# Pinning ScalarE's casts and the gate's tanh to the order of the source in a two-pipe transformer mixer

## The chip, the cores and the metric

The kernel runs on one core of one Trainium2 chip. The metric is device time in microseconds of one launch. The engines named below are TensorE (PE: matmuls and transposes), VectorE (DVE), ScalarE (ACT: casts, exponentials, tanh), GpSimd (POOL) and SyncE (SP, which issues most transfers); each works its own queue from front to back and waits on semaphores for the others.

## The reference

One layer of an encoder over a prompt of 2048 tokens and 8 sample streams of 16 tokens each, 1024 wide:

```python
h   = RMSNorm(x)
z   = h @ w_in     # one combined projection, columns split among head groups
A   = chunk-band attention   # 8 heads x 64: own chunk of 64 and 8 before it, learned bias
B   = mLSTM matrix memory    # 4 heads x 128: exp input gate, sigmoid forget gate, running max
x   = x + RMSNorm(concat(RMSNorm_A(A), sigmoid(o) * headRMSNorm_B(B)) @ w_out)
x   = x + RMSNorm(ConvFFN(RMSNorm(x)))   # up, causal depthwise conv of width 3, GELU gate, down
```

The attention's score is `s = q k / 8 + bias`, masked to the band, then a softmax over the keys and a product with the values. Everything is fp32.

## The kernel before

Each fp32 operand of a matmul is split in two parts: a cast to fp32r on ScalarE gives the high part, a subtraction on VectorE the low part, and three matmuls (`mm3`, lines 95 to 97: high x high, high x low, low x high) give the product. So almost every transfer of an operand is followed by a cast on ScalarE and a subtraction on VectorE before TensorE may read it. Those casts are what the change is about.

The mixers (roughly the first 1100 us of the span; then come the out-projection and the ConvFFN) are built round 28 projection groups, 14 for each half of the prompt, in the order of `GROUPS`: `va` are the attention's values, `qk` its queries and keys, `qb` the queries and keys of the memory, `vo` its values and output gate. A group's weights (512 KB in each of two halves) come through `load_group`. It is called for the next group while the current one runs, and is stepped inside its loop: fetch half 0 into the raw buffer `wraw` (one buffer), cast a quarter (`wi.._h`, L1175) and subtract (`wi.._l`, L1176), then the second quarter, then the same for half 1. A quarter holds two of the eight 128-row blocks of the weights. The results of a group accumulate in two PSUM banks (`ps_mm`), are copied out by ScalarE (L224, L226) and go to DRAM.

Between the matmuls of a group, `pump` inserts steps of two `Pipe`s by a running count of estimated TensorE and VectorE costs. One pipe is the attention: for each head `load_head` fetches queries, keys and values and casts them (`qs` L342, `kh` L346, `vhl` L355). For each tile of 128 queries `att_unit` makes scores `s` (L382, L383), adds the bias and takes the row minimum on VectorE (L393), the exponential on ScalarE (`tmp`, L394), transposes on TensorE (`pt`, L67), casts them on ScalarE (`pth`, L405), subtracts on VectorE (`ptl`, L406), multiplies with the values (`ot`, L418, L419) and adds the two halves of that (`sh` on ScalarE, L424). `attention_sample` does the like for the sample streams against cached keys and values (`qsh` L835, `skh` L852, `svh` L901; fetches `skr`, `svr`). The other pipe is the memory; its `finish_heads` takes the tanh of the output gate (`mvo`, L648).

What sets the order: the program is recorded in the order of the source, and a scheduler then places each engine's instructions. It may place one ahead of others that were written before it. Where `tc.keep_in_program_order(ins)` is called, as it is once in the kernel before,

```python
tc.keep_in_program_order(nc.sync.dma_start(rel[0], I["rel_rev"][:, 0:SQ - 383]))
```

the instruction must stay behind the one recorded just before it on its engine.

Of the kernel before, what the change touches and what calls it, by code (L numbers as in the profile page):

```python
# [12 lines left out]
AF = mybir.ActivationFunctionType  # L13
# [11 lines left out]
DA = 64  # L25
# [19 lines left out]
def hymba_step(ctx: ExitStack, tc: tile.TileContext, I: dict, O: dict):  # L45
    nc = tc.nc
# [22 lines left out]
    def bcast(ap, shape):  # L69
        return ap.broadcast_to(shape)  # L70

    ident = const.tile([P, P], F32, name="ident")
    make_identity(nc, ident)
    nhalf = const.tile([P, 8], F32, name="nhalf")
# [246 lines left out]
    def load_head(s):  # L321
        pair, kg, hh, h, nm = s.pair, s.kg, s.hh, s.h, s.nm
        if kg % 2 == 0:
            nb = pa.tile([P, 640], F32, tag="nb", name=f"nb{nm}", bufs=2)
            nc.sync.dma_start(nb, bias_src(h, P, 640))
            nc.gpsimd.memset(nb[0:64, 576:640], BIG)
            nc.gpsimd.memset(nb[64:128, 0:64], BIG)
            nbs[hh] = nb
        s.nb = nbs[hh]
        rows = slice(hh * 64, hh * 64 + 64)  # L330
        qr = raw_tile(f"qraw{nm}")[:, :512]
        krs = [raw_tile(f"kraw{nm}_{g}")[:, :512] for g in s.segs]
        for r in range(2):
            nc.sync.dma_start(qr[r * 64:r * 64 + 64, :], qTd[pair][kg][rows, :])
        for kr, g in zip(krs, s.segs):
            for r in range(2):
                nc.sync.dma_start(kr[r * 64:r * 64 + 64, :], kTd[pair][g][rows, :])
        yield 0.0, 0.0
        s.kh = pa.tile([P, 1024], F32R, tag="kh", name=f"kh{nm}", bufs=2)
        s.kl = pa.tile([P, 1024], F32R, tag="kl", name=f"kl{nm}", bufs=2)  # L340
        s.qs = pa.tile([P, 512], F32R, tag="qs", name=f"qs{nm}", bufs=2)
        nc.scalar.copy(s.qs, qr)  # L342
        nc.vector.tensor_tensor(s.qs[64:128], qr[64:128], s.qs[64:128], op=ALU.subtract)
        for si, kr in enumerate(krs):
            c = slice(si * 512, (si + 1) * 512)
            nc.scalar.copy(s.kh[:, c], kr)  # L346
            nc.vector.tensor_tensor(s.kl[:, c], kr, s.kh[:, c], op=ALU.subtract)
        new = [g for g in s.segs if g == kg or (h, g) not in vhl]
        vrs = [raw_tile(f"vraw{nm}_{g}")[:, :4 * DA].rearrange("p (a d) -> p a d", a=4) for g in new]
        for vr, g in zip(vrs, new):  # L350
            nc.sync.dma_start(vr, vd[h // 4][g][:, :, (h % 4) * DA:(h % 4 + 1) * DA])
        yield 0.0, 0.6 + 0.6 * len(krs)
        for vr, g in zip(vrs, new):
            t = pa.tile([P, 4, P], F32R, tag="vhl", name=f"vhl{nm}_{g}", bufs=4)
            nc.scalar.copy(t[:, :, 0:DA], vr)  # L355
            nc.vector.tensor_tensor(t[:, :, DA:P], vr, t[:, :, 0:DA], op=ALU.subtract)
            vhl[h, g] = t
        s.v = {g: vhl[h, g] for g in s.segs}
        if kg % 2:
            for g in s.segs:  # L360
                vhl.pop((h, g))
        yield 0.0, 0.34 * len(new)
# [270 lines left out]
    def finish_heads(num, enm, og, h, nch, dst, name):  # L633

        den = num[:, :, 0]
        ad = small.tile([P, 2], F32, tag="ad", name=f"ad{name}")[:, :nch]
        ssq = small.tile([P, 2], F32, tag="mssq", name=f"mssq{name}")[:, :nch]
        nc.vector.scalar_tensor_tensor(ad, den, -1.0, den, op0=ALU.mult, op1=ALU.max)
        nc.vector.tensor_tensor(ad, ad, enm, op=ALU.max)
        for c in range(nch):  # L640
            jk = pm.tile([P, P], F32, tag="wexp", name=f"jk{name}_{c}", bufs=2)
            nc.scalar.activation(jk, num[:, c, 1:DH + 1], AF.Square, accum_out=ssq[:, c:c + 1])
        nc.vector.tensor_tensor(ad, ad, ad, op=ALU.mult)
        nc.vector.scalar_tensor_tensor(ad, ad, DH * EPS, ssq, op0=ALU.mult, op1=ALU.add)
        f = small.tile([P, 2], F32, tag="mf", name=f"mf{name}")[:, :nch]
        nc.gpsimd.tensor_scalar(ad, ad, 1.0 / DH, 0.0, op0=ALU.mult, op1=ALU.add)
        nc.gpsimd.tensor_tensor(f, ad, nhalf[:, :nch], op=ALU.pow)
        nc.scalar.activation(og, og, AF.Tanh, scale=0.5)  # L648
        nc.vector.scalar_tensor_tensor(og, og, 1.0,
                                       hgm[h].unsqueeze(1).broadcast_to([P, nch, DH]),  # L650
                                       op0=ALU.add, op1=ALU.mult)
        for c in range(nch):
            nc.vector.scalar_tensor_tensor(num[:, c, 1:DH + 1], num[:, c, 1:DH + 1], f[:, c:c + 1], og[:, c, :],
                                           op0=ALU.mult, op1=ALU.mult)
        nc.sync.dma_start(dst, num[:, :, 1:DH + 1])
# [163 lines left out]
    def attention_sample(b0, b1):  # L819
        nb = pa.tile([P, LS], F32, tag="nb", name=f"nbs{b0}", bufs=2)  # L820
        qh = pa.tile([P, 4, P], F32R, tag="qs", name=f"qsh{b0}", bufs=2)
# [4 lines left out]
        s = SimpleNamespace()  # L826

        def queries():
            for h in range(HA):
                nc.sync.dma_start(nb[h * DS:(h + 1) * DS, :], bias_src(h, DS, LS))  # L830
            qf = raw_tile(f"qsf{b0}")[:, :512].rearrange("p (a b) -> p a b", a=4)
            for p_ in range(4):
                nc.sync.dma_start(qf[:, p_, :], qTd[p_][4])
            yield 0.0, 0.0
            nc.scalar.copy(qh, qf)  # L835
            nc.vector.tensor_tensor(ql, qf, qh, op=ALU.subtract)
            for z in (zh, zl):
                nc.vector.tensor_scalar(z.rearrange("p (a b) -> p a b", b=P),
                                        tri.unsqueeze(1).broadcast_to([P, 4, P]), 0.0, None, op0=ALU.mult)
            yield 0.0, 1.6  # L840

        def keys(b, p_):
            if p_ == 0 and (b % 4 == 0 or b == b0):
                s.own = pa.tile([P, 4, 64], F32, tag="sh", name=f"own{b}", bufs=1)
                nc.sync.dma_start(s.own, kTs[:, :, b // 4 * 64:b // 4 * 64 + 64])
            kr = raw_tile(f"skr{b}_{p_}")
            nc.sync.dma_start(kr[:, 0:512], I["cache_k"][b, p_])
            nc.gpsimd.tensor_copy(kr[:, 512:LS], s.own[:, p_, b % 4 * DS:b % 4 * DS + DS])
            yield 0.0, 0.0
            kh = pa.tile([P, 1024], F32R, tag="kh", name=f"skh{b}_{p_}", bufs=2)[:, :LS]  # L850
            kl = pa.tile([P, 1024], F32R, tag="kl", name=f"skl{b}_{p_}", bufs=2)[:, :LS]
            nc.scalar.copy(kh, kr)  # L852
            nc.vector.tensor_tensor(kl, kr, kh, op=ALU.subtract)
            if p_ == 0:
                for z, q in ((zh, qh), (zl, ql)):
                    for hh in range(2):
                        rr = slice(hh * 64, hh * 64 + 64)
                        zr = z[rr, hh * DS:(hh + 1) * DS]
                        zd = bass.AP(zr.tensor, zr.offset, [zr.ap[0], [160, 4], [1, DS]])
                        nc.vector.tensor_copy(zd, q[rr, :, b * DS:(b + 1) * DS])  # L860
            yield 0.0, 0.62
            if p_ == 0:
                s.sp = ps_big(f"ss{b}")
            zz = slice(p_ * P, (p_ + 1) * P)
            for o, c in ((0, 0), (512, LS // 2)):
                cs_ = slice(c, c + LS // 2)
                mm3(s.sp[:, o:o + LS // 2], zh[:, zz], zl[:, zz], kh[:, cs_], kl[:, cs_],
                    start=(p_ == 0), stop=(p_ == 3))
            yield 0.66, 0.0
# [24 lines left out]
        def values(b, kk):  # L894
# [3 lines left out]
            yield 0.0, 0.0  # L898
            vh = flat(pa.tile([P, 4, P], F32R, tag="vhl", name=f"svh{b}_{kk}", bufs=4))[:n]
            vl = flat(pa.tile([P, 4, P], F32R, tag="vhl", name=f"svl{b}_{kk}", bufs=4))[:n]  # L900
            nc.scalar.copy(vh, vr)  # L901
            nc.vector.tensor_tensor(vl, vr, vh, op=ALU.subtract)
            yield 0.0, 0.6
            if kk == 0:
# [1 line left out]
            c = slice(kk * P, (kk + 1) * P)  # L906
# [251 lines left out]
    def load_group(gi):  # L1158
# [6 lines left out]
        def steps():  # L1165
            q = n // 2
            for s in range(2):
                raw = pr.tile([P, 1056], F32, tag="wraw", name=f"wi{i}_raw{s}")
                nc.sync.dma_start(raw[:, :q], src[:, s * q:(s + 1) * q])
                yield 0.0, 0.0  # L1170
                yield 0.0, 0.0
                for e in range(2):
                    c = slice(s * q + e * q // 2, s * q + (e + 1) * q // 2)
                    r = raw[:, e * q // 2:(e + 1) * q // 2]
                    nc.scalar.copy(h[:, c], r)  # L1175
                    nc.vector.tensor_tensor(l[:, c], r, h[:, c], op=ALU.subtract)  # L1176
                    yield 0.0, 0.6

# [516 lines left out]
```

## Time and profile before

| | |
|---|---|
| median of 3 runs | 2796.69 us (2793.09 to 2798.26) |
| span of the profiled execution | 2784.7 us |
| time of the profiled execution itself | not listed; the three runs lie 8.4 to 13.6 us above the span |
| mean granted TensorE clock | 0.998 |
| TensorE busy | 2723.8 us (98%), 16587 matmuls |
| VectorE busy | 1876.3 us (67%) |
| ScalarE busy | 1409.1 us (51%), 2836 instructions |
| GpSimd busy | 437.4 us (16%) |
| DMA moved | 486.05 MB |

The span runs from the first instruction to the last. A row of a group gives line, engine, operation, output and inputs, shape and count, then busy microseconds and the mean nanoseconds of one, and then the idle time of the engine before them with what ended it. A row of the waits gives the total, the number and the longest. In a timeline the idle time before an instruction stands in square brackets.

### The profile page before, as it was taken

How to read it: one execution, taken by the hardware profiler on the slowest of the kernel's cores; microseconds unless marked ns; L12 is line 12 of the kernel's file. 1: busy time of each engine (PE TensorE's matmuls, PEld its weight loads, DVE VectorE, ACT ScalarE, POOL GpSimd, SP SyncE). 2: the span in 40 equal slices, each digit the busy share in tenths (PEclk: the TensorE clock that was granted, in tenths of full speed). 3: DMA queues.
4: the chain of work that ended last, by engine and by line, in shares of the span. 5: the costliest groups of instructions: out<-in, count | busy, mean ns of one | idle time of the engine just before them, and what ended most of it. 6: DMA issues, size and time to landing. Idle time of an engine off the chain costs nothing.

```text
span 2784.7 us, 47088 instructions
## 1 busy us (share of the span) xinstructions
PE 2723.8 (98%) x16587; PEld 2548.3 (92%) x16587; DVE 1876.3 (67%) x3447; ACT 1409.1 (51%) x2836; POOL 437.4 (16%) x895
## 2 busy tenths in 40 slices
PE   8999999999999999999999999999999999999998
PEld 7899999998899998888999988899999878999887
DVE  5344455656556668666999986457877864888855
ACT  4355555644356666544454555345455543555543
POOL 1000010212000003244111110011111310222220
PEclk9999999999999999999999999999999999999999
DMA  5544355557555555356655455644544774555585
GB/s 185 155 119 136 103 174 162 164 157 217 162 173 148 144 179 171 107 176 227 187 172 167 167 176 174 219 142 153 160 152 141 276 263 152 172 179 180 192 309 190
DMA packets 311883, 486.05 MB, mean 175 GB/s; under 512 B 55426, under 2 KB 150622, under 8 KB 311518
## 3 DMA queue, kind: packets, MB, share of 16 engines
q1 hardware_dynamic: 271134, 442.92, 50.1%
q10 hardware_dynamic: 38592, 33.83, 3.6%
q0 software_dynamic: 1920, 6.29, 0.6%
q8 instruction: 130, 2.13, 0.3%
q14 instruction: 107, 0.88, 0.1%
HBM read 359.36 MB, written 126.70 MB: 175 GB/s over the span
## 4 chain that ended last, share of the span: by engine, by line
PE 55%; DVE 2%; DMA 1%; issue 1%; ACT 1%; POOL 1%; SPq 0%; DVEq 0%; POOLq 0%; ACTq 0%
PE uec L95 6%; PE uec L96 6%; PE uec L97 6%; PE dn L97 4%; PE dn L96 4%; PE dn L95 4%; PE ua L97 3%; PE ua L95 3%; PE ua L96 3%; PE dnm L97 2%; PE dnm L95 2%; PE dnm L96 2%; PE wo L97 2%; PE wo L95 2%; PE wo L96 2%; PE ub L96 1%
## 5 line engine op out<-in xcount | busy, mean ns | idle before, releaser
L95 PE MATMUL uec<-B,wuh 128*128 128x384 f32 (+1 forms) x720 | 234.9, 328 | 2.2 <-DVE uu L1419 1.1
L96 PE MATMUL uec<-B,wuh 128*128 128x384 f32 (+1 forms) x720 | 235.1, 327 | 0.0
L97 PE MATMUL uec<-B,wul 128*128 128x384 f32 (+1 forms) x720 | 233.9, 327 | 0.0
L1266 DVE TENSOR_TENSOR gl<-gr,gh 128x768 fp32r<-128x768 f32 (+3 forms) x141 | 120.4, 863 | 145.8 <-ACT gh L1265 144.5
L1265 ACT CAST gh<-gr 128x768 fp32r<-128x768 f32 (+3 forms) x141 | 102.0, 735 | 200.1 <-PE dn L96 183.2
L1265 ACT CAST wuh<-wu 128x512 fp32r<-128x512 f32 x255 | 141.7, 617 | 112.1 <-PE uec L96 103.2
L95 PE MATMUL dn<-wdh,gh 128*128 128x512 f32 x466 | 182.4, 391 | 2.3 <-DVE ug L1419 2.3
L96 PE MATMUL dn<-wdl,gh 128*128 128x512 f32 x466 | 183.4, 394 | 0.0
L97 PE MATMUL dn<-wdh,gl 128*128 128x512 f32 x466 | 167.9, 396 | 0.0
L1266 DVE TENSOR_TENSOR wul<-wu,wuh 128x512 fp32r<-128x512 f32 x255 | 164.6, 683 | 2.8 <-DMA x2d<-mx 2.8
L393 DVE CUSTOM_DVE_ANT_0 tmp<-s,nb 128x640 f32<-128x640 f32 (+4 forms) x128 | 94.4, 737 | 96.6 <-PE s L383 94.8
L95 PE MATMUL vo<-wi_h,hT 128*128 128x256 f32 x544 | 155.1, 285 | 0.6 <-DVE mt L199 0.6
L97 PE MATMUL vo<-wi_h,hT 128*128 128x256 f32 x544 | 155.6, 286 | 0.0
L96 PE MATMUL vo<-wi_l,hT 128*128 128x256 f32 x544 | 154.8, 285 | 0.0
L95 PEld LDWEIGHTS uec<-B,wuh 128*128 128x128 f32 x720 | 135.0, 188 | 4.2 <-DVE uu L1419 1.6
L95 PE MATMUL qk<-hT,wi_h 128*128 128x384 f32 (+1 forms) x384 | 128.7, 335 | 7.4 <-ACT qk_st L224 6.6
L96 PEld LDWEIGHTS uec<-B,wuh 128*128 128x128 f32 x720 | 135.2, 188 | 0.2
L97 PEld LDWEIGHTS uec<-B,wul 128*128 128x128 f32 x720 | 135.1, 188 | 0.0
L406 DVE TENSOR_TENSOR ptl<-pt,pth 128x640 fp32r<-128x640 f32 (+4 forms) x128 | 93.6, 737 | 57.1 <-ACT pth L405 56.0
L394 ACT ACTIVATE tmp<-tmp,mn 128x640 f32<-128x640 f32 (+4 forms) x128 | 97.6, 762 | 64.6 <-DVE mn L393 61.9
L96 PE MATMUL qb<-hT,wi_h 128*128 128x384 f32 (+1 forms) x384 | 127.8, 333 | 0.0
L96 PE MATMUL qk<-hT,wi_h 128*128 128x384 f32 (+1 forms) x384 | 127.6, 332 | 0.0
(412 smaller groups left out, 8873.0 us busy)
## 6 DMA issues: line engine op xcount, KB each, us to landing
wu<-in_w_up SPq DMA_DIRECT2D x220, 256.0 KB, 4.1
wu<-wsd SPq DMA_DIRECT2D x176, 256.0 KB, 4.2
wdr<-in_w_down SPq DMA_DIRECT2D x132, 256.0 KB, 5.6
gr<-gd SPq DMA_DIRECT2D x78, 384.0 KB, 3.6
wi_raw<-in_w_in SPq DMA_DIRECT2D x52, 512.0 KB, 4.0
wsd<-ws SPq DMA_DIRECT2D x88, 256.0 KB, 2.8
gd<-g SPq DMA_DIRECT2D x44, 384.0 KB, 3.5
kraw<-kTd SPq DMA_DIRECT2D x112, 128.0 KB, 3.2
```

The lines of the kernel that those rows point to most:

```text
L95: nc.tensor.matmul(out, ah, bh, start=start, stop=False, skip_group_check=onto)
L96: nc.tensor.matmul(out, ah, bl, start=False, stop=False, skip_group_check=onto)
L97: nc.tensor.matmul(out, al, bh, start=False, stop=stop, skip_group_check=onto)
L393: nc.vector.tensor_tensor_reduce(o_, s_, b_, 1.0, 3e38, ALU.add, ALU.min, accum_out=mn)
L394: nc.scalar.activation(tmp[:, :n], tmp[:, :n], AF.Exp, bias=mn, scale=-1.0, accum_out=rsum[:, i % 4, hh:hh + 1])
L406: nc.vector.tensor_tensor(s.ptl[:, sl, qc], ptv, s.pth[:, sl, qc], op=ALU.subtract)
L1265: nc.scalar.copy(h, r)
L1266: nc.vector.tensor_tensor(l, r, h, op=ALU.subtract)
```

## The change

Eight kinds of ScalarE instruction are wrapped in `tc.keep_in_program_order`: the casts of the attention's queries, keys and values, those of the sample's queries, keys and values, the tanh of the output gate, and the weight casts of the projection groups. No instruction is added, removed or altered, and the casts in the ConvFFN are not wrapped. The added line `pin = ...` makes every later line number one higher.

```diff
@@ -69,6 +69,7 @@
 
+    pin = tc.keep_in_program_order
     ident = const.tile([P, P], F32, name="ident")
@@ -339,11 +340,11 @@
         s.qs = pa.tile([P, 512], F32R, tag="qs", name=f"qs{nm}", bufs=2)
-        nc.scalar.copy(s.qs, qr)
+        pin(nc.scalar.copy(s.qs, qr))
         nc.vector.tensor_tensor(s.qs[64:128], qr[64:128], s.qs[64:128], op=ALU.subtract)
...
             c = slice(si * 512, (si + 1) * 512)
-            nc.scalar.copy(s.kh[:, c], kr)
+            pin(nc.scalar.copy(s.kh[:, c], kr))
             nc.vector.tensor_tensor(s.kl[:, c], kr, s.kh[:, c], op=ALU.subtract)
@@ -352,7 +353,7 @@
             t = pa.tile([P, 4, P], F32R, tag="vhl", name=f"vhl{nm}_{g}", bufs=4)
-            nc.scalar.copy(t[:, :, 0:DA], vr)
+            pin(nc.scalar.copy(t[:, :, 0:DA], vr))
             nc.vector.tensor_tensor(t[:, :, DA:P], vr, t[:, :, 0:DA], op=ALU.subtract)
@@ -645,7 +646,7 @@
         nc.gpsimd.tensor_tensor(f, ad, nhalf[:, :nch], op=ALU.pow)
-        nc.scalar.activation(og, og, AF.Tanh, scale=0.5)
+        pin(nc.scalar.activation(og, og, AF.Tanh, scale=0.5))
         nc.vector.scalar_tensor_tensor(og, og, 1.0,
@@ -832,7 +833,7 @@
             yield 0.0, 0.0
-            nc.scalar.copy(qh, qf)
+            pin(nc.scalar.copy(qh, qf))
             nc.vector.tensor_tensor(ql, qf, qh, op=ALU.subtract)
@@ -849,7 +850,7 @@
             kl = pa.tile([P, 1024], F32R, tag="kl", name=f"skl{b}_{p_}", bufs=2)[:, :LS]
-            nc.scalar.copy(kh, kr)
+            pin(nc.scalar.copy(kh, kr))
             nc.vector.tensor_tensor(kl, kr, kh, op=ALU.subtract)
@@ -898,7 +899,7 @@
             vl = flat(pa.tile([P, 4, P], F32R, tag="vhl", name=f"svl{b}_{kk}", bufs=4))[:n]
-            nc.scalar.copy(vh, vr)
+            pin(nc.scalar.copy(vh, vr))
             nc.vector.tensor_tensor(vl, vr, vh, op=ALU.subtract)
@@ -1172,7 +1173,7 @@
                     r = raw[:, e * q // 2:(e + 1) * q // 2]
-                    nc.scalar.copy(h[:, c], r)
+                    pin(nc.scalar.copy(h[:, c], r))
                     nc.vector.tensor_tensor(l[:, c], r, h[:, c], op=ALU.subtract)
```

Order of ScalarE before, where the attention of half 0 runs under the end of group va1 and the start of qk2 (`wi5` are the weights of the later group qk3, `tmp0_6` is head 0, query tile 6, `kh2_0` and `qs2_0` are the keys and queries of head 2):

```order
L394 ACTIVATE tmp0_5_1745,rsum0_1_1692<-tmp0_5_1745,mn0_5_1746 128x640
L405 COPY pth0_4_1762<-pt0_4_1764 128x5x128
L224 COPY va1_0_st16_2126<-va1_0_16_2050 128x256
L1175 COPY wi5_h5_2130<-wi5_raw0_2145 128x512 x2
L275 DMA vs_77<-va1_0_st16_2126 128x256
L277 DMA out_v_sample<-va1_0_st16_2126 128x256
L394 ACTIVATE tmp0_6_1789,rsum0_1_1692<-tmp0_6_1789,mn0_6_1790 128x640
L226 ACTIVATE qk2_0_st0_0_2197<-qk2_0_0_0_2132 128x384
L405 COPY pth0_4_1762<-pt0_5_1793 128x5x128
L239 DMA qTd2_0_104<-qk2_0_st0_0_2197 128x384
L1175 COPY wi5_h5_2130<-wi5_raw1_2286 128x512 x2
L346 COPY kh2_0_1924<-kraw2_0_0_1870 128x512
```

Order of ScalarE after, later in the program, where qk3 already runs (`qs3_0`, `kh3_0`, `vhl3_0_0` are the operands of head 3):

```order
L425 COPY sh1_6_2114<-ot1_6_2101 64x256
L343 COPY qs3_0_2119<-qraw3_0_2067 128x512
L347 COPY kh3_0_2117<-kraw3_0_0_2068 128x512
L406 COPY pth2_0_2167<-pt2_0_2169 128x128
L395 ACTIVATE tmp2_1_2150,rsum1_0_2094<-tmp2_1_2150,mn2_1_2151 128x256
L356 COPY vhl3_0_0_2164<-vraw3_0_0_2124 128x4x64
L395 ACTIVATE tmp2_2_2188,rsum1_0_2094<-tmp2_2_2188,mn2_2_2189 128x384
L406 COPY pth2_0_2167<-pt2_1_2192 128x2x128
L425 COPY sh2_0_2228<-ot2_0_2222 64x256
L395 ACTIVATE tmp2_3_2218,rsum1_0_2094<-tmp2_3_2218,mn2_3_2219 128x512
L406 COPY pth2_2_2231<-pt2_2_2233 128x3x128
L1176 COPY wi5_h5_2130<-wi5_raw0_2145 128x512
```

Before, all four casts of wi5 stand in two pairs a group ahead of their use; after, one stands there (row 155) and the other three at rows 200, 203 and 213, the second behind the attention of heads 2 and 3.

Order of TensorE before, in group qk3 of half 0 (`qk3_0_0_2` is one of its accumulators, `s2_2` the scores of head 2, tile 2, `ao` the transposed output of an earlier pair):

```order
L95 MATMUL qk3_0_0_2_2749<-hT0_2_632,wi5_h5_2130 128x384
L96 MATMUL qk3_0_0_2_2749<-hT0_2_632,wi5_h5_2130 128x384
L382 MATMUL s2_2_2185<-kh2_0_1924,qs2_0_1926 128x384
L383 MATMUL s2_2_2185<-kl2_0_1925,qs2_0_1926 128x384
L67 MATMUL ao0_1_2156<-ident_69,attT0_1_1839 128x128 x2
L97 MATMUL qk3_0_0_2_2749<-hT0_2_632,wi5_l5_2131 128x384
```

Order of TensorE after, in the same group, behind its first twelve matmuls:

```order
L67 MATMUL ao0_1_2156<-ident_69,attT0_1_1839 128x128 x2
L67 MATMUL pt2_1_2192<-ident_69,tmp2_1_2150 128x128 x2
L419 MATMUL ot2_0_2222<-pth2_0_2167,vhl2_0_0_1954 128x256
L383 MATMUL s2_3_2215<-kh2_0_1924,qs2_0_1926 128x512
L384 MATMUL s2_3_2215<-kl2_0_1925,qs2_0_1926 128x512
L420 MATMUL ot2_0_2222<-ptl2_0_2168,vhl2_0_0_1954 128x256
L419 MATMUL ot2_0_2222<-pth2_0_2167,vhl2_0_0_1954 128x128
L420 MATMUL ot2_0_2222<-ptl2_0_2168,vhl2_0_0_1954 128x128
L67 MATMUL pt2_2_2233<-ident_69,tmp2_2_2188 128x128 x3
L67 MATMUL pt2_3_2262<-ident_69,tmp2_3_2218 128x128 x4
L96 MATMUL qk3_0_0_0_2576<-hT0_0_349,wi5_h5_2130 128x384
L97 MATMUL qk3_0_0_0_2576<-hT0_0_349,wi5_h5_2130 128x384
```

Before, the scores and transposes of head 2 stand singly among matmuls of qk3; after, 30 rows of attention (1025 to 1054) stand together between the group's first twelve matmuls and its next ones.

Order of ScalarE before, near the start, in group qk0 (`qk0_0_st1_1` is its second key copy):

```order
L620 ACTIVATE pks_924<-pks_924 4x128 x3
L224 COPY qk0_0_st1_0_1068<-qk0_0_1_0_1000 128x384
L239 DMA kTd0_0_78<-qk0_0_st1_0_1068 128x384
L342 COPY qs0_0_1290<-qraw0_0_1263 128x512
L224 COPY qk0_0_st1_1_1110<-qk0_0_1_1_1071 128x384
L239 DMA kTd0_0_78<-qk0_0_st1_1_1110 128x128
L239 DMA kTd0_1_79<-qk0_0_st1_1_1110 128x256
```

Order of ScalarE after, at the same place:

```order
L621 ACTIVATE pks_924<-pks_924 4x128 x3
L1176 COPY wi2_h2_828<-wi2_raw0_843 128x512
L225 COPY qk0_0_st1_0_1068<-qk0_0_1_0_1000 128x384
L240 DMA kTd0_0_78<-qk0_0_st1_0_1068 128x384
L1176 COPY wi2_h2_828<-wi2_raw1_976 128x512 x2
L225 COPY qk0_0_st1_1_1110<-qk0_0_1_1_1071 128x384
L240 DMA kTd0_0_78<-qk0_0_st1_1_1110 128x128
L240 DMA kTd0_1_79<-qk0_0_st1_1_1110 128x256
L225 COPY qk0_0_st1_2_1160<-qk0_0_1_2_1114 128x384
```

The cast `qs0_0` no longer stands ahead of that copy; it comes at row 81.

## The prediction

> **What bounds the kernel now.** I read the span and the windows first. In the windows the second figure is TensorE's busy time, and the last three are granted clock, DMA share and GB/s.
>
> ```profile
> span 2784.7 us, 47088 instructions
> ```
>
> ```profile
> 0.00:60.00 60.00, 46.37 (x334) 44.63 (x335) 33.33 (x65) 28.88 (x50) 9.99 (x33) 1.00 0.52 172
> 60.00:120.00 60.00, 53.29 (x308) 50.68 (x307) 19.00 (x69) 17.87 (x42) 2.08 (x7) 0.97 0.64 182
> 120.00:260.00 140.00, 140.00 (x970) 138.94 (x969) 67.97 (x143) 72.19 (x163) 0.98 (x7) 1.00 0.41 124
> 260.00:500.00 240.00, 239.35 (x1759) 235.12 (x1759) 125.91 (x301) 125.87 (x303) 16.74 (x51) 1.00 0.48 143
> 500.00:760.00 260.00, 247.14 (x1731) 233.05 (x1730) 149.44 (x420) 122.30 (x312) 47.74 (x136) 1.00 0.59 180
> 760.00:1000.00 240.00, 239.81 (x1835) 237.17 (x1835) 144.25 (x331) 144.20 (x348) 13.86 (x43) 1.00 0.53 157
> 1000.00:1100.00 100.00, 97.67 (x684) 89.43 (x683) 77.87 (x168) 69.20 (x173) 19.25 (x37) 1.00 0.58 179
> ```
>
> All pinned casts lie before about 1100 us. TensorE is busy 1063.6 of those 1100 us, so it idles 36.4 us, of which 13.6 in the first 60. Between 120 and 500 us it idles 0.65 us, between 760 and 1000 us 0.2 us: TensorE is the bound, and these stretches can only lose. Next, what TensorE waits for up to 1100 us (total, times, longest), and what ScalarE waits for there:
>
> ```profile
> PE hT_pt L67 <- DVE xr L219: 9.9, 3, 8.2
> PE qk L95 <- ACT qk_st L224: 6.6, 2, 3.3
> ```
>
> ```profile
> ACT svh L901 <- DMA svr<-in_cache_v: 34.3, 14, 5.1
> ...
> ACT wi_h L1175 <- DMA wi_raw<-in_w_in: 28.4, 23, 3.9
> ACT mvo L648 <- DMA mvo<-vobd: 27.9, 22, 2.6
> ...
> ACT skh L852 <- DMA skr<-in_cache_k: 20.3, 11, 5.5
> ...
> ACT qs L342 <- DMA qraw<-qTd: 17.4, 4, 11.0
> ...
> ACT vhl L355 <- DMA vraw<-vd: 12.5, 12, 3.1
> ```
>
> The change pins just these instructions. ScalarE runs its queue in order, and stands 140.8 us (the sum of the six) behind a cast or tanh whose transfer has not landed, yet TensorE hardly notices: it has projection matmuls to run meanwhile. It has them because the weights come early. The timeline at the start of group qk3 of the first half shows how early. By the order, the first row is the second pair of qk3's four weight casts (wi5), the next is qk2's last output copy, and the last is qk3's first one:
>
> ```profile
> 157.37 1.14 ACT L1175 CAST wi_h<-wi_raw 128x512 fp32r<-128x512 f32 x2 [1.11 <-DMA qTd<-qk_st]
> ...
> 184.72 0.47 ACT L224 COPY qk_st<-qk 128x384 f32<-128x384 f32 x1
> ...
> 190.99 0.49 ACT L226 ACTIVATE qk_st<-qk 128x384 f32<-128x384 f32 x1
> ```
>
> So all four casts were done some 26 us before qk3 began.
>
> **The change part by part.** No instruction is added or dropped; the terms are order and waits. A pinned instruction stays behind the ScalarE instruction written before it, so it can no longer float ahead.
>
> *A, weight casts behind the attention in the mixers.* In the changed order the first of wi5's casts still comes a whole group ahead (ScalarE row 155 after, 147 before), but the second stands at row 200, behind 44 rows of attention and copies, and the third and fourth at 203 and 213. qk3 begins with a quarter of its weights: its two accumulators (two banks only) take 12 matmuls, and then TensorE has nothing but attention until row 200 is through. The prices of what stands in ScalarE's queue, and of VectorE's subtraction behind a weight cast:
>
> ```profile
> L1175 ACT CAST wi_h<-wi_raw 128x512 fp32r<-128x512 f32 x104 | 59.6, 620 | 34.4 <-DMA wi_raw<-in_w_in 23.6 <-PE qb L96 3.8 <-DMA vobd<-vo_st 2.3
> ...
> L346 ACT CAST kh<-kraw 128x512 fp32r<-128x512 f32 x54 | 31.8, 618 | 16.6 <-DMA kraw<-kTd 9.0 <-PE s L382 4.0 <-PE s L383 3.4
> ...
> L424 ACT COPY sh<-ot 64x256 f32<-64x256 f32 x57 | 21.1, 369 | 25.0 <-PE ot L419 21.8 <-DMA qkbd<-qb_st 2.1
> ...
> L355 ACT CAST vhl<-vraw 128x256 fp32r<-128x256 f32 x38 | 15.2, 401 | 14.2 <-DMA vraw<-vd 12.5 <-PE ot L419 1.3 <-PE sot L97 0.4
> ...
> L394 ACT ACTIVATE tmp<-tmp,mn 128x384 f32<-128x384 f32 x8 | 4.9, 618 | 8.8 <-DVE mn L393 8.7
> ...
> L394 ACT ACTIVATE tmp<-tmp,mn 128x256 f32<-128x256 f32 x8 | 4.1, 511 | 1.9 <-DVE mn L393 1.7
> L405 ACT CAST pth<-pt 128x384 fp32r<-128x384 f32 x8 | 3.8, 479 | 0.2
> ...
> L405 ACT CAST pth<-pt 128x256 fp32r<-128x256 f32 x8 | 2.9, 364 | 4.7 <-PE pt L67 4.7
> ...
> L405 ACT CAST pth<-pt 128x128 fp32r<-128x128 f32 x8 | 2.1, 264 | 1.1 <-ACT qk_st L224 0.9
> ```
>
> ```profile
> L1176 DVE TENSOR_TENSOR wi_l<-wi_raw,wi_h 128x512 fp32r<-128x512 f32 x104 | 68.3, 691 | 36.0 <-ACT wi_h L1175 35.6
> ```
>
> The queue's hand-over, TensorE's prices and the landing times:
>
> ```profile
> 81.98 0.62 ACT L342 CAST qs<-qraw 128x512 fp32r<-128x512 f32 x1 [10.99 <-DMA qraw<-qTd]
> 82.50 0.47 ACT L224 COPY qk_st<-qk 128x384 f32<-128x384 f32 x1
> ```
>
> ```profile
> 1900.00:2000.00 100.00, 100.00 (x576) 100.00 (x575) 77.81 (x115) 50.16 (x81) 12.46 (x28) 1.00 0.48 153
> ```
>
> ```profile
> 1104.98 0.12 PE ot L419
> ...
> 1109.50 0.55 PE pt L67 x5
> ```
>
> ```profile
> wi_raw<-in_w_in SPq DMA_DIRECT2D x52, 512.0 KB, 4.0
> ...
> svr<-in_cache_v SPq DMA_DIRECT2D x32, 256.0 KB, 4.5
> ```
>
> Back to back, a ScalarE row starts 0.1 us before the last one's listed end (0.52 after a row of 0.62). A 384-column matmul costs TensorE 100/576 = 0.174 us, one of 256 columns 0.12, a transpose 0.11.
>
> First stretch, from the end of ot1_6 to ot2_0. ScalarE: sh1_6 0.369, qs3_0 and kh3_0 at 0.618, pth2_0 0.264, tmp2_1 0.511, vhl3_0_0 0.401, tmp2_2 0.618, pth2_0's second part 0.364: 3.76 us, less 0.7 for seven hand-overs, 3.1. TensorE has s2_1 (2 x 0.12), s2_2 (2 x 0.174) and five transposes (0.55): 1.14. It idles 2.0, with the signals between engines about 2.2. Five smaller waits for an exponential or a pth of the same run were found in the same way, 0.5 to 0.75 each, 3.1 together. Second stretch: pth2_2 0.479, the second weight cast 0.620, its subtraction 0.691, then the second raw half may be fetched, since there is one raw buffer: 4.0. Its cast (0.620) stalls ScalarE, and behind it stand sh2_2 0.369, three 128x512 casts 1.854, pth3_0 0.264 and tmp3_1 0.511, which pt3_1 on TensorE needs: 9.4 us (hand-overs taken to cancel against the signals between engines), against 26 matmuls of 384 columns (4.5), 8 of 256 (1.0) and 9 narrow ones (0.9): 3.0 idle. Edge of qk3: 2.2 + 3.1 + 3.0 = 8.3, by the whole count 8.5.
>
> Other edges, by the same count over the new order: qb0 2.6, vo0 3.9, qb1 1.0, vo1 8.6, vo2 4.9, qb3 2.4, and in the second half vo0 4.4, vo1 9.0, vo2 1.6, vo3 2.7. The two big ones, vo1, are a chain: the second raw half lands 4.0 after it is asked for, its cast holds twelve ScalarE rows, and the sample's svr fetch (4.5) may begin only after the subtraction behind them. In all 49.6, so **A = +50**. From below: if ScalarE keeps up, or the transfers are asked for earlier than I count, half, +25; from above: the same count applied to the kernel before gave 14.0 us where the windows show 22.8 outside the first 60 us, a factor of 1.6, so +80.
>
> *B, the start.* The first group's casts fall behind the Squares and hT copies of the first tiles; the first row of TensorE's waits (8.2 us at once, for the norm) is already there. Counted: +4 (0 to +6).
>
> *C, a stall that goes.* The 10.99 us wait of the qs cast stood in front of qk0's second key copy, and TensorE waited for that copy (6.6 us in two waits). Pinned, qs0_0 stands at ScalarE row 81 and that copy at 59. What is late next is the key transfers themselves, so I take **C = -6** (-8 to -3).
>
> *D, the tanh, the sample's casts and the clock.* The tanh and the sample casts keep their transfers; TensorE's edge at vo1 already holds the sample's share, the rest is hidden under projections: 0. The clock after an idle spell:
>
> ```profile
> 104.00:108.00 4.00, 1.21 (x7) 0.89 (x6) 0.00 (x0) 0.00 (x0) 0.00 (x0) 1.00 0.95 293
> 108.00:109.00 1.00, 0.45 (x1) 0.45 (x2) 0.00 (x0) 0.48 (x1) 0.00 (x0) 0.75 0.70 152
> 109.00:113.00 4.00, 4.00 (x18) 4.00 (x18) 0.29 (x1) 0.81 (x3) 0.77 (x2) 0.64 0.44 100
> ```
>
> A gap of about 4 us cost 0.25 x 1 + 0.36 x 4 = 1.7 us of granted clock. The new gaps are mostly 0.5 to 3 us with matmuls between; two of them may reach it: **D = +3** (0 to +17).
>
> The sum is 50 + 4 - 6 + 3 = 51. On the profiled execution's span of 2784.7 that gives 2835.7; the runs' median of 2796.69 lies 12.0 above the span (the execution's own time is listed nowhere), so **2848 us**.
>
> **The rivals.** *The clock falls at each edge.* For it: the rows above. Against it: only matmuls standing still nearly all of 4 us brought it on. At ten edges 17 instead of 3: 2862, and with A at its upper end 2892. [...]
>
> *The casts cover themselves (no change).* If VectorE and ScalarE catch up during the first 12 matmuls and the attention's own, A shrinks to 0 to 7 and C pays for most of it: 2784.7 + 7 + 4 - 6 + 12 = 2802 at most, 2795 with none. Against it: 3.1 us of ScalarE on 1.14 of TensorE stand in fixed order, and this can't shrink by timing.
>
> *Faster: ScalarE stops sitting behind transfers.* With the casts back at their written place, their raw tiles have landed, and ScalarE gains up to 140.8 us. TensorE can gain only its idle time outside the start, 22.8, and of that only what ScalarE causes, C and about 2 more: 2789. It decides if the edges of A stay under 4 us in all; the 0.65 us of idle between 120 and 500 us speaks against any gain there.
>
> *Half of A.* ScalarE's waits at the edges hide behind one another: 2784.7 + 25 + 4 - 6 + 1 + 12 = 2821.
>
> **How the numbers follow.** The forecast holds 0.62, half of A 0.17, the clock at each edge (or fetches held up further along SyncE's queue, at a like price) 0.12, no change 0.04, faster 0.05. A measurement can tell 0.2%, 5.6 us, from no change. Range 2812 to 2900: the low end is half of A with B and D at 0 and C at -8, 2814, the high one A at 80 with B at 6, C at -3 and D at 17, 2897, both rounded outwards. Chances: faster 0.05, same 0.04, slower 0.91.
>
> **What would show it.** Right: TensorE idle of 40 to 60 us more before 1100 us, in clusters at the first matmuls of qk3, vo0, vo1 and vo2 in both halves; new rows among TensorE's waits for pth L406 and tmp L395 and for the weight cast L1176; the span after 1340 us unchanged; the two qk_st waits gone. Wrong: windows 120 to 500 and 760 to 1000 still under 1 us idle, or the loss lying after 1340 us, or a granted clock under 0.95 over whole groups.

## The result and the profile after

The changed kernel takes 2860.89 us (median of 4 runs, 2858.66 to 2872.43), the kernel before 2794.89 us (4 runs, 2790.93 to 2798.26). That is a ratio of 1.0243 (95% interval 1.0226 to 1.0261), 66 us slower. The forecast was 2848 us in a range of 2812 to 2900.

The page and the cores of the changed kernel, and its windows, cut so that each holds about the work of the window shown of before (some 7020 matmuls up to 1070 us here, some 6940 up to 1000 us there):

```profile
span 2859.1 us, 47125 instructions
...
PE 2752.2 (96%) x16587; PEld 2562.5 (90%) x16587; DVE 1879.1 (66%) x3447; ACT 1408.3 (49%) x2836; POOL 442.7 (15%) x895
```

```profile
core 0: 2859.1 us, clock 0.992
```

```profile
0.00:60.00 60.00, 42.69 (x305) 40.53 (x306) 29.63 (x45) 27.08 (x44) 11.63 (x33) 1.00 0.49 160
60.00:120.00 60.00, 51.42 (x280) 48.24 (x279) 18.86 (x77) 14.98 (x35) 2.65 (x7) 0.94 0.49 151
120.00:280.00 160.00, 148.73 (x1013) 142.58 (x1012) 78.86 (x174) 82.95 (x193) 1.28 (x9) 1.00 0.40 116
280.00:540.00 260.00, 245.88 (x1741) 236.26 (x1740) 131.94 (x342) 124.14 (x313) 23.09 (x76) 0.99 0.48 142
540.00:820.00 280.00, 272.27 (x1889) 260.38 (x1888) 138.30 (x359) 121.70 (x290) 40.90 (x109) 0.98 0.55 169
820.00:1070.00 250.00, 240.57 (x1792) 234.62 (x1792) 148.07 (x341) 146.70 (x356) 15.10 (x45) 0.98 0.50 147
1070.00:1170.00 100.00, 92.80 (x630) 84.24 (x629) 76.72 (x168) 65.93 (x169) 20.27 (x39) 0.98 0.59 178
...
1412.00:2860.00 1448.00, 1426.70 (x7748) 1321.00 (x7746) 1087.72 (x1716) 718.92 (x1208) 239.72 (x469) 1.00 0.57 187
```

The span grew by 74.4 us. TensorE's idle time (span less busy) grew from 60.9 to 106.9, by 46.0. From 120 to 280 us it is 11.3 now and in the next window 14.1; the kernel before had 0.65 in all from 120 to 500 us. TensorE's busy time grew by 28.4 with the same 16587 matmuls: the mean clock fell from 0.998 to 0.992, which is 0.008 x 2859 = 23 us of lost clock against 0.002 x 2785 = 6, so 17 of the 28 (each good to some 1.4 us, as the clock has three digits). The last window, the ConvFFN, has the same busy time as before (1426.70 against 1426.79).

Some of the new waits of TensorE, with one, the second, whose like stands in the list of before (there at the key copy, L224); and the wait of ScalarE's weight casts for their transfers:

```profile
PE qb L96 <- ACT wi_h L1176: 5.1, 3, 2.5
PE qk L96 <- ACT qk_st L227: 4.6, 1, 4.6
...
PE va L96 <- ACT wi_h L1176: 3.2, 2, 2.7
...
PE ot L419 <- ACT pth L406: 3.0, 5, 1.3
...
PE vo L96 <- ACT wi_h L1176: 2.8, 5, 1.2
```

```profile
ACT wi_h L1176 <- DMA wi_raw<-in_w_in: 76.5, 34, 9.0
```

ScalarE waits 76.5 us for raw weights (28.4 before). Some of its other waits for transfers did go, as the rival "Faster" of the prediction had it: for the sample's values it stands 2.0 us (34.3 before), for the prompt's queries 1.2 (17.4), and for the gate's `mvo` no row is left (27.9); for the prompt's values it rose to 25.3 (12.5). No gain of TensorE's came with that.

The place that the prediction worked out, the edge of qk3 in the first half, on ScalarE and then on TensorE (start, duration, instruction, idle before it):

```profile
207.31 0.48 ACT L406 CAST pth<-pt 128x384 fp32r<-128x384 f32 x1
207.68 0.62 ACT L1176 CAST wi_h<-wi_raw 128x512 fp32r<-128x512 f32 x1
208.20 0.59 ACT L406 CAST pth<-pt 128x512 fp32r<-128x512 f32 x1
...
213.00 0.62 ACT L1176 CAST wi_h<-wi_raw 128x512 fp32r<-128x512 f32 x1 [2.52 <-DMA wi_raw<-in_w_in]
...
219.33 0.60 ACT L1176 CAST wi_h<-wi_raw 128x512 fp32r<-128x512 f32 x1
```

```profile
207.34 0.66 PE L67 MATMUL pt<-ident,tmp 128*128 128x128 f32 x4 [0.92 <-ACT tmp L395]
208.36 0.45 PE L96 MATMUL qk<-hT,wi_h 128*128 128x384 f32 x1 [0.36 <-ACT wi_h L1176]
213.67 0.44 PE L96 MATMUL qk<-hT,wi_h 128*128 128x384 f32 x1 [1.44 <-ACT wi_h L1176]
217.41 0.41 PE L67 MATMUL pt<-ident,tmp 128*128 128x128 f32 x2 [0.98 <-DVE ptl L407]
```

```profile
200.00:220.00 20.00, 14.04 (x81) 10.71 (x80) 12.70 (x36) 12.29 (x34) 0.00 (x0) 1.00 0.38 107
```

The chain is there row by row: pth, second weight cast, fetch (ScalarE stands 2.52 us for it), third cast, and the matmul of qk3 behind it. TensorE idles 6.0 us in these 20 (8.5 counted).

The other edges can be read in much the same way, by summing the gaps between TensorE's rows from the first matmul of a group to that of the next. In the first half they hold, with the forecast in brackets: qb0 3.1 (2.6), vo0 3.8 (3.9), qb1 0.5 (1.0), vo1 5.5 (8.6), vo2 1.9 (4.9), qb3 2.5 (2.4); in the second half vo0 5.9 (4.4), vo1 5.1 (9.0), vo2 0.6 (1.6), vo3 3.8 (2.7). In the kernel before, the same groups hold 2.4 us together.

### The profile page after: what moved, and what is told of

The parts are those of the page before. It is cut to its first block, busy times and chain, and to the rows that moved or that the text cites. A ratio compares the mean times of both kernels' runs of the same rounds, so it can differ in the third digit from the quotient of the medians.

```text
span 2859.1 us, 47125 instructions
## 1 busy us (share of the span) xinstructions
PE 2752.2 (96%) x16587; PEld 2562.5 (90%) x16587; DVE 1879.1 (66%) x3447; ACT 1408.3 (49%) x2836; POOL 442.7 (15%) x895
## 4 chain that ended last, share of the span: by engine, by line
PE 53%; DVE 3%; DMA 2%; issue 1%; ACT 1%; POOL 1%; SPq 0%; DVEq 0%; POOLq 0%; ACTq 0%
PE uec L96 6%; PE uec L97 6%; PE uec L98 6%; PE dn L98 4%; PE dn L97 4%; PE dn L96 4%; PE ua L98 3%; PE ua L97 3%; PE ua L96 3%; PE dnm L98 2%; PE dnm L96 2%; PE dnm L97 2%; PE wo L98 2%; PE wo L96 2%; PE wo L97 2%
## 5 line engine op out<-in xcount | busy, mean ns | idle before, releaser
L1177 DVE TENSOR_TENSOR wi_l<-wi_raw,wi_h 128x512 fp32r<-128x512 f32 (+1 forms) x112 | 76.4, 690 | 92.5 <-ACT wi_h L1176 91.5
L98 PE MATMUL qk<-hT,wi_l 128*128 128x384 f32 (+1 forms) x384 | 127.1, 332 | 0.0
```

Of the source, the lines that this page charges most:

```text
L98: nc.tensor.matmul(out, al, bh, start=False, stop=stop, skip_group_check=onto)
```

## The experiments

The idle time in this table is the span less TensorE's busy time, the lost clock is (1 - mean clock) times the span; both are from the profiled execution. The time is the median of the runs. A ratio is taken to runs of the kernel before made beside the kernel in question, whose medians are 2792.90 to 2794.89.

| kernel | us | ratio to before (95%) | TensorE idle | lost clock |
|---|---|---|---|---|
| before | 2794.89 | | 60.9 | 6 |
| changed | 2860.89 | 1.0243 (1.0226 to 1.0261) | 106.9 | 23 |
| weight casts alone pinned | 2847.78 | 1.0191 (1.0164 to 1.0219) | 96.4 | 20 |
| all but the weight casts | 2813.27 | 1.0068 (1.0047 to 1.0090) | 72.9 | 22 |
| changed, weight steps written first | 2851.87 | 1.0206 (1.0180 to 1.0233) | 102.4 | 31 |
| changed, raw weights by quarters | 2834.15 | 1.0143 (1.0120 to 1.0167) | 86.9 | 26 |
| weight casts of vo1 alone | 2832.92 | 1.0144 (1.0130 to 1.0158) | 85.5 | 20 |
| attention's casts alone | 2805.47 | 1.0044 (1.0029 to 1.0058) | 72.2 | 11 |
| sample's casts alone | 2819.57 | 1.0090 (1.0074 to 1.0106) | 81.2 | 11 |
| tanh alone | 2811.13 | 1.0059 (1.0036 to 1.0082) | 68.3 | 22 |
| first two heads' casts alone | 2790.32 | 0.9986 (0.9978 to 0.9995) | 62.7 | 11 |

**Weight casts alone, and all but these.** In the first kernel only the last `pin` of the diff is kept, in the second only the other seven:

```diff
 # weight casts alone: the other seven lines as before, for instance
-            pin(nc.scalar.copy(s.kh[:, c], kr))
+            nc.scalar.copy(s.kh[:, c], kr)
 # all but these
-                    pin(nc.scalar.copy(h[:, c], r))
+                    nc.scalar.copy(h[:, c], r)
```

> Only the weight casts of the projection groups are pinned; the other seven kinds float as before. Theory W (weights that come late leave TensorE with nothing but attention): the loss stays for the greater part, because the casts of a group still stand behind the attention written before them; counting the new order as in the prediction gives TensorE 56 us of waits against 69 for the whole change and 14 for the kernel before, so about 42 of idle and 8 to 14 of half clock: 2840 to 2855. Rival Q (ScalarE, held in written order, sits behind the transfers of queries, keys, values and gates): these casts float again, so the loss is mostly gone: 2795 to 2810.

> The seven other kinds are pinned, the weight casts float as before. Theory W: TensorE keeps its early weights; the count gives 24 us of waits against 14 before, all of it after 940 us: 2800 to 2808, and no idle TensorE between 120 and 500 us. Rival Q: the loss stays, 2835 to 2861.

2847.78 and 2813.27 us. The two windows 60 to 120 and 120 to 500 us, first of the weight casts alone, then of all but these:

```profile
60.00:120.00 60.00, 53.12 (x285) 50.08 (x283) 20.84 (x82) 16.12 (x38) 1.39 (x6) 0.94 0.61 169
120.00:500.00 380.00, 362.71 (x2555) 348.86 (x2554) 197.50 (x472) 197.77 (x480) 19.01 (x68) 0.99 0.45 133
```

```profile
60.00:120.00 60.00, 56.66 (x344) 53.56 (x343) 20.69 (x73) 19.26 (x47) 1.81 (x7) 1.00 0.61 187
120.00:500.00 380.00, 376.66 (x2685) 371.32 (x2686) 188.80 (x435) 193.88 (x457) 17.66 (x58) 1.00 0.45 135
```

The weight casts alone bring 1.9 of the 2.4%, with 17.3 us of idle TensorE between 120 and 500; without them it is 3.3. The first time lies in the range given for theory W. That is for the late weights and against the rival of a ScalarE held up by all its transfers. But the second kernel is 5 us slower than the range given for it, and its 3.3 us between 120 and 500 were to be none: idle grew by 12.0 us in all, the lost clock by 17. In its first window TensorE idles 3.3 us instead of 6.7.

**The weight steps written a group earlier.**

```diff
-                ahead.append(next(split, (0.0, 0.0)))
+                ahead += [next(split, (0.0, 0.0)) for _ in range(8 if u == 0 else 1)]
```

> All pins of the change, but a group's eight weight steps (two fetches, four casts) are written in the first unit of the group before it rather than one for each unit. Theory W: it is the written place that ties the casts to the attention's lag; written a whole group earlier they are done before the group begins, so the idle of 160 to 420 us and of 680 to 860 us goes (the count shows none there); ScalarE sits behind the second half's transfer instead, and the count puts 40 us of new waits after 900 us, where attention has been pushed: 2830 to 2850, with the windows 120 to 500 nearly full. Rival Q: the pins of the attention are unchanged, so those windows stay as idle as in the changed kernel, 20 us and more.

2851.87 us, 1.9 above the range of theory W. The windows 120 to 500 and 500 to 1000:

```profile
120.00:500.00 380.00, 379.16 (x2720) 373.88 (x2719) 189.78 (x438) 194.19 (x460) 19.74 (x58) 1.00 0.47 139
500.00:1000.00 500.00, 487.93 (x3548) 470.97 (x3548) 259.13 (x646) 241.13 (x583) 53.55 (x159) 1.00 0.54 161
```

With every pin in place TensorE is full again, 0.8 us idle in 380, as in before. So the place at which the weight casts are written, behind attention that runs later than it is written, opened the edges. The time is not won, only 9 us of 66: the idle time lies at the end of the mixers now, 46.8 us of it with a clock of 0.96 in the window below (8.9 us in 1000 to 1340 of before), where attention is left without projections beside it. Waits there were expected from the order, 40 us of them. This kernel shows what opened the edges, then, but not what closing them would be worth.

```profile
1000.00:1409.00 409.00, 362.25 (x2007) 309.37 (x2006) 291.78 (x533) 213.57 (x509) 116.20 (x172) 0.96 0.49 154
```

**Raw weights by quarters.** The raw buffer's two halves are fetched and cast in turn (`q` is now a quarter of the columns, `rs` the list of fetched quarters, `keep[0]` one raw tile kept for all groups):

```diff
-            for s in range(2):
-                raw = pr.tile([P, 1056], F32, tag="wraw", name=f"wi{i}_raw{s}")
-                nc.sync.dma_start(raw[:, :q], src[:, s * q:(s + 1) * q])
+            for s in range(5):
+                if s < 4:
+                    rs.append(keep[0][:, s % 2 * 528:s % 2 * 528 + q])
+                    nc.sync.dma_start(rs[s], src[:, s * q:(s + 1) * q])
...
+                if s:
+                    c = slice((s - 1) * q, s * q); r = rs[s - 1]
```

> All pins of the change, but the raw weights are fetched in quarters (256 KB) into the two halves of the raw buffer, so the fetch of the next quarter needn't wait until the one before it is cast. If the chain of cast, subtraction and 4.0 us of fetch through the single raw buffer carries the loss (the second stretch of the prediction), half or more of it goes: 2815 to 2830. If it is the written place behind the attention, whatever the fetch does, little goes; the count gives 60 against 69: 2848 to 2858.

2834.15 us, 27 less than the changed kernel and outside both ranges. ScalarE's wait for raw weights:

```profile
ACT wi_h L1176 <- DMA wraw<-in_w_in: 27.7, 17, 6.8
```

It is back to what it was in before (28.4), and with it some 40% of the loss went, not the eighth that the count gave. The chain of cast, subtraction and fetch through the one raw buffer weighs more than the count gave it. Between 120 and 500 us TensorE still idles 16.6 us (22.9 in the changed kernel); that the written place carries this rest is what the kernel before this one speaks for, and was not tried together with quarters.

**Group vo1 alone.**

```diff
-                    pin(nc.scalar.copy(h[:, c], r))
+                    (pin if GROUPS[gi] == "vo1" else (lambda x: x))(nc.scalar.copy(h[:, c], r))
```

The other seven kinds float.

> Only the weight casts of group vo1 (once in each half) are pinned, everything else floats. Theory W: one late group is enough to open TensorE; the count over the new order puts 25 us of waits at the start of vo1 in the first half and 4 in the second, and 4 more after 960 us, against 14 us in all before: 2818 to 2838, with the idle between 280 and 360 us of the span and half-clock spells there. Rival: the loss of the changed kernel needs all groups behind the attention at once, a single one is made up for by the groups round it: 2790 to 2800.

2832.92 us. The windows of 20 us from 320:

```profile
320.00:340.00 20.00, 16.83 (x115) 14.71 (x114) 11.50 (x24) 11.50 (x23) 0.00 (x0) 1.00 0.14 37
340.00:360.00 20.00, 14.93 (x97) 13.11 (x97) 12.39 (x33) 10.28 (x26) 2.41 (x8) 0.91 0.39 112
360.00:380.00 20.00, 16.68 (x97) 13.28 (x95) 14.30 (x45) 12.32 (x37) 4.14 (x14) 0.91 0.69 213
```

The time is within the range of theory W. One late group (twice in the program) costs more than half of the whole loss. In these 60 us, at the start of vo1, TensorE idles 11.6 us (25 were counted, from 280 to 360), with a clock of 0.91 in the last two windows. The groups do not add up. It may be that where all are late, a group's lateness is partly the next one's lead; this was not tried.

**The other pins, each kind by itself.** Only `qs`, `kh` and `vhl`; only `qsh`, `skh` and `svh`; only the tanh.

> Only the casts of the prompt's queries, keys and values (qs, kh, vhl) are pinned. The 20 us that the seven kinds together cost must be somewhere: if the prompt's attention carries them, 2806 to 2815; if the sample's casts do, 2795 to 2802 here (the count: 21 us of waits against 14 before, all after 940 us).

> Only the casts of the sample's queries, keys and values (qsh, skh, svh) are pinned. If these carry the 20 us of the seven kinds, 2806 to 2815 and half-clock spells between 420 and 760 us, where the sample's attention runs; if not, 2795 to 2802 (the count: 20 us of waits against 14).

> Only the output gate's tanh is pinned. The prediction put it at 0; the count gives 16.5 us of waits against 14. No difference: 2791 to 2800. If every disturbance of the planner's order costs some tenths of a per cent, as the sample's casts alone cost more than all seven kinds together, 2803 to 2815.

2805.47, 2819.57 and 2811.13 us. The first lies just under its upper range, the second above both of its ranges, and the tanh in its second one. Each costs 0.4 to 0.9%, all seven kinds together 0.7%, so they don't add up either, and no one kind carries the 20 us. The prediction put the tanh at 0, and the count saw only 2.5 us of waits in it. Its window 500 to 760 us:

```profile
500.00:760.00 260.00, 246.83 (x1696) 232.49 (x1695) 143.90 (x415) 118.71 (x307) 47.04 (x132) 0.97 0.59 175
```

TensorE is as busy as in before (247.14) but does 35 matmuls fewer, at a clock of 0.97 instead of 1.00: what this order loses there is clock, not idle time. Pinning one kind makes the scheduler place most of what follows anew (with the tanh alone, ScalarE's order is that of before up to 268 us, and from there to 1340 most of its instructions stand at other places); that the new places fall worse is seen, why each does is not settled.

**The first two heads' casts alone.**

```diff
+        first = pin if h < 2 and kg == 0 else lambda x: x
...
-        nc.scalar.copy(s.qs, qr)
+        first(nc.scalar.copy(s.qs, qr))
```

and the like for `kh` and `vhl`.

> Only the casts of the first two heads' first load (kg 0) are pinned, so that the 10.99 us wait for the first queries no longer stands in front of a key copy of qk0; later in the program the order is that of before. Term C of the prediction by itself: with the seven kinds pinned TensorE's idle between 60 and 120 us fell from 6.7 to 3.3 and the half-clock spell there went (1.7), so 5 us: 2786 to 2790, ratio 0.998. If the next late transfer takes the wait's place, as in the whole change, no difference: 2791 to 2796.

2790.32 us (11 runs, against 16 of the kernel before beside them), between the two ranges; ratio 0.9986 (0.9978 to 0.9995): 4 us faster than before, and the fastest of all. The window in question:

```profile
60.00:120.00 60.00, 57.29 (x343) 54.81 (x342) 21.46 (x74) 19.37 (x46) 1.81 (x7) 0.97 0.65 189
```

TensorE idles 2.7 us there instead of 6.7, and from the 300th instruction on ScalarE's order in the mixers is that of before. Over the whole span the profiled execution doesn't show the gain (62.7 us idle against 60.9; it took 2794.71 us, more than the median), so the gain rests on the medians, and the window is the likely place. Term C was in part a true price of the wait, but not a gain of the whole change.

**What a gap costs in clock.** In the kernel before, nothing pinned, the up-projection of two blocks gets artificial waits, in the second version from an accumulator (`e`) that is done twelve matmuls earlier (an estimated 2 us, at 0.174 us each by the window of before in the prediction) and with f modulo 7:

```diff
+            if b < 2 and f >= 2:
+                for _ in range(f % 9):
+                    nc.scalar.copy(x1[:, :n], was[:, :n])
+                for o in (a, d_, e, c) if f % 9 else ():
+                    transpose(o[:, :P], x1[:, :P])
+            was = c
             product(P1, w[0], a)
```

> The kernel before with nothing pinned; in the up-projection of the first two blocks, where TensorE is otherwise full, each of 40 rounds f (2 to 21) first makes TensorE wait for f modulo 9 ScalarE copies in a row (0 to 8, about 0.4 us each; the copies and four transposes are extra work whose output is overwritten). So 36 gaps of about 0.6 to 3.4 us stand alone among full matmuls, some 67 us of idle. Theory S (short gaps do it): spells of half clock follow gaps well under 3 us, as after 4 of the changed kernel's gaps of 1.5 to 2.5 us; with a spell of 3.4 us for about half of the gaps, 18 x 1.7 = 31 us: near 2893. [...]

> As the gap ladder, but the copies read an accumulator that is done twelve matmuls (2 us) earlier, and there are 0 to 6 of them, so that the gaps fill the range from about 1 to 5 us that the first ladder skipped: there, 14 isolated gaps of under 2.2 us (and some 70 of 0.65) brought no spell of half clock, and 34 of 35 of 2.98 us and more did. Theory S (short gaps do it): isolated gaps of 1.3 to 2.6 us bring spells in about half of the cases, as in the mixers. Rival: an isolated gap needs about 2.5 to 3 us; then the spells after gaps of 1.3 to 2.5 us in the mixers come from the thin work round them, not from the gap alone.

3152.87 us, and 3127.72 in one run. The time given for the first was missed by far, since most gaps came out longer than planned (up to 8.0 us in the second: the copies stand in ScalarE's queue behind weight casts and the convolution's activations), but the gaps themselves can be read. By TensorE's rows of both kernels in the ConvFFN, none of 16 gaps of 0.89 to 2.15 us was followed by a spell of half clock, and all gaps of over 3.8 us were. Between these, length does not decide: in the second kernel one of 2.37 us was followed by a long spell, one of 3.37 us by none. The windows round these two:

```profile
2330.00:2336.00 6.00, 3.14 (x16) 2.83 (x17) 6.00 (x10) 5.18 (x9) 1.07 (x2) 1.00 0.86 249
2336.00:2346.00 10.00, 7.17 (x27) 6.66 (x26) 7.85 (x10) 3.61 (x6) 0.96 (x3) 0.52 0.59 189
```

```profile
2072.00:2076.00 4.00, 0.63 (x6) 0.59 (x6) 3.96 (x7) 3.29 (x6) 1.33 (x2) 1.00 0.46 143
2076.00:2080.00 4.00, 4.00 (x25) 4.00 (x24) 1.71 (x2) 1.33 (x2) 0.19 (x1) 1.00 0.40 141
```

In the changed kernel the eight spells before the end of the span last 3.413, 6.827 or 10.240 us by the clock's records in the trace, and follow gaps shorter than the ladder's. Behind a gap of 2.15 us that ends at 810.9:

```profile
811.00:821.00 10.00, 10.00 (x36) 8.21 (x37) 5.22 (x8) 3.35 (x6) 1.22 (x2) 0.50 0.53 184
```

Ten us at half clock, 5 us lost, for 2.15 us of waiting. So neither theory holds as it stood. Among full matmuls no gap under 2.37 us brought a spell, but in the mixers of the changed kernel 5 spells followed the 17 gaps of 1.2 to 2.5 us between 60 and 1110 us, the shortest of these five gaps being 1.5 us.

The traces show what goes before a spell. In each of the thirteen, all spells begin on one grid of stretches of 3.413 us; in the changed kernel the one at the span's end begins 2747.73 us behind the first, 805 stretches of 3.4133 us, and each of those between lies within 0.002 of a whole number of them. Two gaps of 2.15 us in the changed kernel, one that ends at 259.3 and the one that ends at 810.9, in stretches of its grid:

```profile
254.38:257.80 3.41, 2.52 (x16) 2.03 (x14) 2.35 (x7) 1.62 (x3) 0.00 (x0) 1.00 0.88 263
257.80:261.21 3.41, 1.96 (x15) 1.93 (x16) 1.23 (x3) 1.44 (x3) 0.40 (x3) 1.00 0.48 138
261.21:264.62 3.41, 3.41 (x28) 3.27 (x27) 1.92 (x3) 2.28 (x4) 0.00 (x0) 1.00 0.00 0
```

```profile
807.34:810.75 3.41, 1.46 (x10) 1.12 (x8) 0.00 (x0) 0.49 (x1) 0.00 (x0) 1.00 0.74 257
810.75:814.16 3.41, 3.22 (x10) 2.31 (x10) 2.52 (x4) 1.72 (x4) 1.22 (x2) 0.50 0.34 120
```

The first gap is split between two stretches, in which TensorE is still busy 74 and 57% of the time, and nothing follows. The second falls almost whole into one stretch (43% busy), and the next runs at half clock. Over all thirteen traces, from 30 us on and without the last 50 us of each, 140 of 142 full-clock stretches in which TensorE was busy for less than 45% were followed by half clock, and 10 of 10167 in which it was busy for 55% or more; the kernel before and the changed one by themselves give 7 of 8, and 1 of 1573. So, by these traces, the sum of all waits in a stretch counts, long or short, and where the grid happens to lie.

## Why the prediction was right, and which terms were off

The direction, the cause and the range held: the weight casts alone bring four fifths of the loss, and writing them earlier fills the edges. Of the signs that it named, the idle time lies at the groups foretold, the new waits for the weight casts, `pth` and `tmp` (1.6 us) are there, and the ConvFFN is unchanged. TensorE's idle time up to about the same work (1170 us here, 1100 in before) grew by 39 us, just under the 40 to 60 named, and the `qk_st` waits did not go. By its terms, on the spans (+74.4 against the sum of 51):

- *A, +50.* The mechanism was right, edge by edge, and the size a quarter too large. Idle time grew by 46.0 in all; less the first 120 us (5.6) and the ConvFFN (2.5, to the ends of the spans) that is 38. At qk3 6.0 us were measured for 8.5. The 0.2 us in it for the signals between engines were the author's estimate; the rows show 0.05 for one of these, from the listed end of the third cast (213.62) to its matmul (213.67). Within A the share of the raw buffer was too small: by the count, quarters should have saved 9 us of waits, and 27 us of time went. ScalarE's casts waited 76.5 us for their transfers; why the count fell short of that is not settled.
- *B, +4.* Measured +3.7: 17.3 us idle in the first 60 instead of 13.6. There TensorE waits 2.7 us for a weight cast and 3.5 for VectorE's hT, rows that before does not have.
- *C, -6.* Wrong as a term of this change, in two steps. The 6.6 us were two waits, and only the first (3.24, up to 83.0) followed the queries' cast; the second (3.34, up to 108.6) ended with a copy before which ScalarE had stood idle for 7.3 us, and no queries' cast stood there. And though the first queries' cast no longer stands there, the step "what is late next is the key transfers themselves" failed. Idle in 60 to 120 us rose from 6.7 to 8.6. On ScalarE stand instead a raw weight cast and the memory's exponential, which the new order places ahead of qk's output copies:

```profile
85.14 1.14 ACT L1176 CAST wi_h<-wi_raw 128x512 fp32r<-128x512 f32 x2 [8.99 <-DMA wi_raw<-in_w_in]
...
107.65 0.40 ACT L690 ACTIVATE w<-mb,colsp 128x128 f32<-128x128 f32 x1 [7.69 <-POOL mb L674]
...
109.18 0.47 ACT L227 ACTIVATE qk_st<-qk 128x384 f32<-128x384 f32 x1
```

```profile
109.70 0.69 PE L96 MATMUL qk<-hT,wi_h 128*128 128x384 f32 x1 [4.56 <-ACT qk_st L227]
```

  Two `w` rows stand ahead of that copy, and the order was not followed that far. Alone, with most of the order kept, the term is worth 4 us.
- *D, +3.* Mis-sized: 17, the price written for the rival "the clock falls at each edge", and its upper bound here. "Only matmuls standing still nearly all of 4 us brought it on" was read from one gap, and misread: that gap was 3.34 us (the rows show 1.21 us of matmuls in the 4), and it filled 97% of one stretch of the grid, 105.09 to 108.51, while the gap of 3.24 us before it was split between two and brought nothing. What this reading missed is that shorter waits in one stretch add up: the spell at 899.50 us of the changed kernel follows waits of 1.65 and 1.34 us, and in the stretch that holds most of both TensorE is busy for 0.74 of 3.41 us, 22%:

```profile
896.09:899.50 3.41, 0.74 (x5) 0.53 (x5) 3.41 (x7) 3.12 (x8) 0.00 (x0) 1.00 0.47 127
899.50:902.91 3.41, 3.36 (x14) 3.36 (x15) 2.58 (x6) 0.89 (x3) 0.00 (x0) 0.50 0.85 235
```

  A single wait of 2.15 us, the one that ends at 810.9, was enough as well. In both spells the clock was 0.50.
- The remaining 11 us of busy time have no wait or lower clock in the records; what they are was not settled.
- *The 12.0 us above the span.* They were not overhead. The profiled execution of the changed kernel took 2860.84 us with a span of 2859.1, 1.7 above it, and in every later profiled execution it was 1.7 to 2.0. So the span of 2784.7 belongs to an execution some 8 us faster than the usual run, and the medians differ by 66, not 74. With the 12.0 added, the forecast is in effect the usual run and 51 more, which has to be held against the 66.

The forecast of 51 came near 66 by terms that partly made up for one another, and in that it was lucky: A was 12 too much, C and D together 22 too little, and the remaining 11 us stood in no term.

## What to carry to other kernels

A cast that stages an operand far ahead must not be tied to the written place of work that runs late: here the weights then arrived with that work, and TensorE, whose projections should have hidden it, idled 22.9 us between 120 and 500 us (0.65 before). When a change opens many short waits on TensorE, price the clock with them: here 46 us of added waiting brought 17 us of lost clock, and a reordering that added only 12 us of waiting brought as much. What to look for in these traces is a stretch of 3.41 us in which TensorE works for less than 45% of the time: half clock followed 140 of 142 of these. Pinning is best kept to the one place where the trace shows an early instruction blocking the queue: two heads' casts, pinned alone, gave the only gain of this study, 4 us of 2794.

## What was not expected of the hardware

Spells of half clock last 3.4 us or a multiple (up to 13.7 in the ladder) and begin on a grid of 3.413 us. In the mixers of the changed kernel five of them began after waits of 1.5 to 2.5 us, though none of 16 waits of 0.89 to 2.15 us among full matmuls brought one. Where the grid lies differs between executions: its first boundary in the span comes 2.69 us after the start in the kernel before, 1.80 us in the changed one. The kernel with the tanh alone has the order of before up to 268 us and idles there near 80 and 105 us as before does, yet three stretches of half clock follow instead of one (mean clock 0.91 from 60 to 120 us against 0.97). Of 16 runs of the kernel before, the three with a mean clock of 0.995 took 2796.54 to 2797.86 us, the two with 0.998 2792.05 and 2792.86. So a difference of some us between two single executions says little.
